# Two-layer hybrid attention trunk: up products with both halves of the hidden rows in one matmul, compression copies for two groups, first transposes in the output banks

## The chip, the cores and the metric

The kernel runs on one core of one Trainium2 chip. The metric is the device time of one execution in microseconds; lower is better.

## What is computed

Two layers (DEPTH = 2) over 256 tokens of width 1024, float32 in and out. Each layer has two attention mixers that share one input projection, a merge, and a gated feed-forward block with a causal convolution of width 3 after its up projection:

```python
def hybrid_layer(x, positions, ...):
    h = rms_norm(x, attn_pre_gain)
    u = h @ w_in
    (qa, ka, va, qb, kcb, vcb, ksb, vsb, kwb, vwb, g_nsa, g_a, g_b) = jnp.split(u, offsets, axis=-1)
    o_a = swa_sink_attention(qa, ka, va, attn_sinks)          # rotary qa, ka; window 128
    kc = compress(kcb, ...); vc = compress(vcb, ...)           # blocks of 32 rows, stride 16, small MLP
    o_b = nsa_attention(qb_raw, qb_rot, kc, vc, ks, vs, kw, vw, gates)
    mixed = jax.nn.sigmoid(g_a) * (o_a @ w_branch_a) + jax.nn.sigmoid(g_b) * (o_b @ w_branch_b)
    x = x + rms_norm(mixed @ w_out, attn_post_gain)
    h = rms_norm(x, ffn_pre_gain)
    return x + rms_norm(conv_ffn(h, ffn_w_up, ffn_conv_w, ffn_conv_b, ffn_w_down), ffn_post_gain)

def conv_ffn(h, w_up, conv_w, conv_b, w_down):
    u = h @ w_up                                               # 1024 -> 2 x 2816
    c = conv_b + sum of conv_w[k] * (u shifted by 2 - k tokens)
    a, val = jnp.split(c, 2, axis=-1)
    return (jax.nn.gelu(a, approximate=True) * val) @ w_down
```

## The kernel before

**Numbers in two parts.** Each operand of a large product is split into a high part in the matmul's rounded float32 format (`wh`, `hh`, `gh`) and a low part, the rest (`wl`, `hl`, `gl`). A product is the sum of three: high by high, high by low, low by high (`mm3`, lines 388 to 390, and the three matmuls of `up`, lines 1065 to 1067). ACT makes a high part by a copy (helper `copy`, line 114), DVE the low part by a subtraction (helper `sub`, line 117). The weights stream from memory through `Stream`: a staging tile `st`, then `wh` and `wl`, with four slots each; `W.next` hands out the next weight and makes those a little ahead.

**Order.** The program is written with a scheduler that orders each engine's instructions on a modelled time, by the order in which they are written, and that sets all waits; some stretches (`manual_schedule`) keep the written order. Work that comes between products is put off by ticks: `later(n, fn)` calls `fn` n products later, with the delays in `DL` and `PLAN`. Each engine runs its own instructions strictly in their order.

**PSUM.** Eight banks in four tags of two: `mm`, `T`, `S` and `O`. Projections use `mm` and `S`, transposes `T`, scores `S`, the attention outputs (`values`, tiles `OB`) and one token block of the down product `O`.

**Attention.** `in_tile` makes the projection in nine column tiles, for two blocks of 128 tokens (`t`); when a block of a tile is done a `fin_...` function takes it over. `q_rot`, `q_raw` and `k_rot` make stacks `stk` with high and low parts (with the rotary embedding by `rope`), and `stack_T` transposes a stack on PE into a `T` bank, four matmuls on line 515, from where ACT copies it to qA, qB, qR, kA, kS or kW. `fin_c` copies the rows to be compressed to `kvd`, one copy for keys and one for values; `cmp_blocks` transposes them (line 728) into one `T` bank and makes high and low parts in `M`, for two parities and two groups `g`: four ACT copies and four DVE subtractions for keys and as many for values. `cmp_hidden` multiplies `M` with the compression weights (line 760). `Unit.scores` (line 637), `probs_T` (line 676) and `values` (lines 708 to 710) are the attention proper; `out_T` splits an output into `OT`. Queries, outputs `OT` and the hidden pair `hp` of the feed-forward block share the tag `q8` with three buffers; the tile of one early weight uses it too.

**Feed-forward.** There are 22 pairs `j` of 128 gate and 128 value columns. Pairs 0 and 1 are made in another way (`up_first`). From pair 2 on, `up(j, half, ...)` makes the 128 columns of one half for all 256 tokens in half a bank, 24 matmuls of 256 columns; `act_gate(j)` makes the convolution (`conv`: one ACT operation, line 1048, and two DVE operations, lines 1051 and 1052), the gelu, the product (line 1073) and its high and low parts `gh`, `gl`; `down(j - 2, t)` adds the pair two before to the result. The tiles of 256 columns come from the tag `k1` with eleven buffers. In layer 0 the last pairs also make weights of the next layer (`early`).

Of the kernel before, what the change touches and what calls it, by code (L numbers as in the profile page):

```python
# [16 lines left out]
P = 128  # L17
# [35 lines left out]
DL = {'qa0': 2, 'qa1': 13, 'ka': 6, 'qb0': 8, 'qr0': 8, 'qb1': 2, 'qr1': 4, 'cb0': 1, 'cb1': 3, 'ks': 1, 'kw': 6, 'pT': (3, 3, 2), 'pv': 4, 'hT': 1, 'ge': 3, 'pj': 4, 'cT': 5, 'cv': 9, 'yT': 1, 'h0': 5, 'h1': 4, 'uf': 0, 'x0': 3, 'x1': 3}  # L53
WARM = (6, 2, 3)
FIRST = [(0, 0), (1, 0), (0, 1), (1, 1), (0, 2), (1, 2), (0, 3), (1, 3)]
EARLY = {4: ("sg", 2), 6: ("sg", 2), 8: ("kB", 1)}
# [9 lines left out]
def tile_hybrid_trunk(  # L66
# [146 lines left out]

    TAGS = {"kB": 1, "sg": 2, "q8": 3}
    W = Stream()
# [227 lines left out]
    def attn_layer(l, xp, rs, gains, first, order, last_T):  # L443
# [66 lines left out]

        def stack_T(stk, dst, key, n):
            def fn():
                b = bank("T")
                for h in range(4):
                    pe.transpose(b[:, h * P:(h + 1) * P].bitcast(F32R), stk[:, h * P:(h + 1) * P], ident_r)
                copy(dst, b.rearrange("p (h c) -> p h c", h=4) if n == 0 else b.rearrange("p (g s c) -> p g s c", g=2, s=2))
                done.add(key)
            return fn

        def q_rot(qT, t, h0, src, key, delays, exp_after=None):  # L520
            d = rope(src, t, True, 4 * len(delays))
            for i, delay in enumerate(delays):
                stk = k2(F32R)
                sv = stk.rearrange("p (h a d) -> p h a d", h=4, a=2)
                di = d[:, 4 * i:4 * i + 4, :]
                hi = copy(sv[:, :, 0, :], di)
                if exp_after is not None:
                    with tc.issue_after(hi.ins):
                        table(exp_after)
                    exp_after = None  # L530
                sub(sv[:, :, 1, :], di, r32(sv[:, :, 0, :]))
                h = h0 + 4 * i
                later(delay, stack_T(stk, qT[:, h:h + 4, t * P:(t + 1) * P], (key[0], t, h // 4), 0))

# [10 lines left out]
        def k_rot(t, src, dsts):  # L545
            d = rope(src, t, False, 2 * len(dsts))
            for i, (kT, key, delay) in enumerate(dsts):
                stk = k2(F32R)
                sv = stk.rearrange("p (g s a d) -> p g s a d", g=2, s=2, a=2)
                kb = d[:, 2 * i:2 * i + 2, None, :].to_broadcast([P, 2, 2, 64])  # L550
                copy(sv[:, :, 0], kb)
                sub(sv[:, :, 1], kb, r32(sv[:, :, 0]))
                later(delay, stack_T(stk, kT[:, :, :, t * P:(t + 1) * P], key, 1))

# [7 lines left out]

        qA, qB, qR = big8("q8", 3), big8("q8", 3), big8("q8", 3)
        kA = ap_.tile([P, 2, 2, T], F32R, tag="kA", name=nm("kA"))
# [20 lines left out]
        def fin_c(t, b):  # L585
            q_rot(qB, t, 4, heads(b, 0, 4), ("qB", t, 1), (DL["qb1"],))
            q_raw(qR, t, 4, heads(b, 0, 4), ("qR", t, 1), DL["qr1"])
            for kd in range(2):
                kvd[t][kd] = k2()
                dv = kvd[t][kd][:, 0:256].rearrange("p (g a d) -> p g a d", g=2, a=2)  # L590
                src = heads(b, 256 + kd * 128, 2)
                copy(dv, src[:, :, None, :].to_broadcast([P, 2, 2, 64]), scale=rs[t])
            if t == 1:
                later(DL["cb0"], lambda: cmp_blocks(0))
                later(DL["cb1"], lambda: cmp_blocks(1))
# [116 lines left out]
        def out_T(br, g):  # L712
            if OT[br] is None:
                OT[br] = big8("q8", 3)
            bv = OB[br][g].rearrange("p (k c) -> p k c", k=2)
            ho = OT[br][:, g * 2:g * 2 + 2, :]
            copy(ho, bv)
            sub(OT[br][:, 4 + g * 2:6 + g * 2, :], bv, r32(ho))


        def cmp_blocks(kd):
# [4 lines left out]
            for g in range(2):  # L726
                for t in range(2):
                    pe.transpose(b[:, (g * 2 + t) * P:(g * 2 + t + 1) * P], kvd[t][kd][:, g * P:(g + 1) * P], ident)
            bv = b.rearrange("p (g c pr two) -> p two pr g c", g=2, c=16, two=2)
            for par in range(2):  # L730
                rr = slice(par * 64, par * 64 + 64)
                for g in range(2):
                    ho = M[rr, :, 0:16, g]
                    copy(ho, bv[rr, par, :, g, :])
                    sub(M[rr, :, 0:16, 3 + g], bv[rr, par, :, g, :], r32(ho))
            o = R_POS + (l * 2 + kd) * 16
# [224 lines left out]
        branch(1)  # L961
        return yp

    def out_layer(l, yp, gains, order):
        gains["ffn_pre"] = gain_tile(ffn_pre_gain, l)
# [29 lines left out]
        for k in range(1, 8):  # L995
            if k < 6:
                W.make(first + k + 2)
            product(0, [k])
        hp = big8("q8", 3), big8("q8", 3)
        g, r = norm_a(res[0], gp)  # L1000
# [26 lines left out]
        scaled(1, r)  # L1027
        return hp, [lambda: t4_of(xg[1], hp, 1, 0), lambda: (t4_of(xg[1], hp, 1, 1), low())]


    def ffn_layer(l, hp, gains, last, order, last_T):
        hh, hl = hp
        gains["ffn_post"] = gain_tile(ffn_post_gain, l)
# [10 lines left out]

        def conv(b, jj, half, then=None):
            c = k1()
            u = b[:, half * T:(half + 1) * T]
            act.activation(c, u, AF.Identity, bias=cb(l, jj), scale=cw(l, 2, jj))
            if then:
                then()  # L1050
            dve.scalar_tensor_tensor(c[:, 1:T], u[:, 0:T - 1], cw(l, 1, jj), c[:, 1:T], ALU.mult, ALU.add)
            dve.scalar_tensor_tensor(c[:, 2:T], u[:, 0:T - 2], cw(l, 0, jj), c[:, 2:T], ALU.mult, ALU.add)
            return c

        up_bank, up_w, gs, wdn = {}, {}, {}, {}

        def up(j, half, c0, c1):
# [11 lines left out]
        def act_gate(j):  # L1069
            b = up_bank.pop(j)  # L1070
            ca, cv = conv(b, j, 0), conv(b, 22 + j, 1)
            act.activation(ca, ca, AF.Gelu_apprx_tanh)
# [58 lines left out]
        for j in range(2, NJ - 1):  # L1131
            for half in range(2):
                part(lambda: up(j, half, 0, T))
            act_gate(j)
# [12 lines left out]
        part(lambda: up(j, 0, 0, T))  # L1147
        ca = conv(up_bank.pop(j), j, 0)
        act.activation(ca, ca, AF.Gelu_apprx_tanh)
        up_bank[j] = bank("mm")  # L1150
        part(lambda: up(j, 1, 0, T))
        nxt = None if last else [early[l + 1, "in", c] for c in range(4)]
        cv = conv(up_bank.pop(j), 22 + j, 1, None if last else lambda: lows.append(W.high(nxt[2])))
        dve.tensor_tensor(ca, ca, cv, ALU.mult)
# [103 lines left out]
    for l in range(DEPTH):  # L1258

        yp = attn_layer(l, xp, rs, gains, l == 0, order, last_T)  # L1260
        hp, last_T = out_layer(l, yp, gains, order)
        xp, rs, last_T = ffn_layer(l, hp, gains, l == DEPTH - 1, order, last_T)
    idle(50)
# [78 lines left out]
```

## Time and profile before

| | us |
|---|---|
| median of 3 runs | 775.21 |
| lowest and highest | 775.03, 776.46 |
| the profiled execution | 774.85 |
| its span, first to last instruction | 772.8 |

In the profiled execution the span is 772.8 us of the 774.85; the rest lies around it. The busy times of the engines over the span are:

| engine | busy us | share | instructions |
|---|---|---|---|
| PE (matmul) | 756.8 | 98% | 4742 |
| PEld (weight load) | 677.0 | 88% | 4742 |
| DVE | 611.1 | 79% | 1181 |
| ACT | 497.9 | 64% | 951 |
| POOL | 26.9 | 3% | 52 |

All times of the trace are counted from the start of the span. In time order it holds, per layer, the attention stage (in layer 0 until about 165 us), the branch products, merge and output projection (until about 200 us), and the feed-forward block (until about 392 us); layer 1 follows in the same way. Matmuls are pipelined: one matmul's duration overlaps the next one's, so the pitch from start to start tells what a matmul costs, not its duration.

### The profile page before, as it was taken

To read this page: it belongs to the slowest core of one execution; us is meant where nothing else is said; L and a number is where in the kernel's file an instruction comes from. 1 tells how busy PE (TensorE), PEld (TensorE's weight loads), DVE (VectorE), ACT (ScalarE), POOL (GpSimd) and SP (SyncE) were. 2 spreads that over 40 slices of the span, in tenths; PEclk is the share of its full clock that TensorE was granted. 3 is DMA by queue.
4 is the path that set the end of the run, shared out by engine and by line. 5 is a ranking of instruction groups with operands and counts; after the bars stand their busy time and mean duration, and the time that the engine had idled before them with its cause. 6 is when DMAs were issued, how large, how long until landed. Compare 5 with 4: busy or idle time off the path is not lost.

```text
span 772.8 us, 12863 instructions
## 1 busy us (share of the span) xinstructions
PE 756.8 (98%) x4742; PEld 677.0 (88%) x4742; DVE 611.1 (79%) x1181; ACT 497.9 (64%) x951; POOL 26.9 (3%) x52
## 2 busy tenths in 40 slices
PE   8999999999999999999999999999999999999995
PEld 6888898888899999999878889988888999999994
DVE  7998898687687777777787989985967877777774
ACT  6686986755665555665566979776565655566552
POOL 3000001000000000000010000010010000000000
PEclk9999999999999999999999999999999999999998
DMA  8633265355655556766335224644655656566621
GB/s 333 198 107 122 63 205 190 137 179 178 195 202 182 187 189 191 230 221 209 132 131 157 89 79 136 210 149 148 206 189 163 185 184 191 185 192 219 196 82 55
DMA packets 42345, 131.25 MB, mean 170 GB/s; under 512 B 5375, under 2 KB 5931, under 8 KB 42283
## 3 DMA queue, kind: packets, MB, share of 16 engines
q1 hardware_dynamic: 41707, 129.39, 51.6%
q10 hardware_dynamic: 576, 1.05, 0.4%
q8 instruction: 37, 0.61, 0.3%
q14 instruction: 25, 0.20, 0.1%
HBM read 129.37 MB, written 1.05 MB: 169 GB/s over the span
## 4 chain that ended last, share of the span: by engine, by line
PE 86%; ACT 8%; DVE 3%; issue 1%; DMA 1%; POOL 0%; SPq 0%; DVEq 0%; POOLq 0%; ACTq 0%
PE mm L388 6%; PE mm L389 6%; PE mm L390 6%; PE S L388 5%; PE S L390 5%; PE S L389 5%; PE mm L1067 5%; PE mm L1066 5%; PE mm L1065 5%; PE T L1066 5%; PE T L1065 5%; PE T L1067 5%; PE O L389 4%; PE O L388 4%; PE O L390 4%; ACT k L649 2%
## 5 line engine op out<-in xcount | busy, mean ns | idle before, releaser
L117 DVE TENSOR_TENSOR wl<-st,wh 128x1024 fp32r<-128x1024 f32 (+2 forms) x214 | 253.2, 1184 | 89.4 <-ACT wh L114 86.8
L114 ACT ACTIVATE wh<-st 128x1024 fp32r<-128x1024 f32 (+2 forms) x214 | 219.1, 1027 | 158.1 <-PE mm L1066 36.8
L1065 PE MATMUL mm<-q,wh 128*128 128x256 f32 x336 | 95.1, 283 | 0.0
L1067 PE MATMUL mm<-q,wl 128*128 128x256 f32 x336 | 95.0, 283 | 0.0
L1066 PE MATMUL mm<-q,wh 128*128 128x256 f32 x336 | 95.0, 283 | 0.0
L388 PE MATMUL mm<-wh,x 128*128 128x512 f32 (+2 forms) x240 | 89.8, 374 | 0.1
L389 PE MATMUL mm<-wl,x 128*128 128x512 f32 (+2 forms) x240 | 88.2, 368 | 0.0
L390 PE MATMUL mm<-wh,x 128*128 128x512 f32 (+2 forms) x240 | 88.0, 367 | 0.0
L1066 PE MATMUL T<-q,wh 128*128 128x256 f32 x304 | 86.0, 283 | 0.0
L1067 PE MATMUL T<-q,wl 128*128 128x256 f32 x304 | 86.0, 283 | 0.0
L1065 PE MATMUL T<-q,wh 128*128 128x256 f32 x304 | 85.9, 283 | 0.0
L1065 PEld LDWEIGHTS mm<-q,wh 128*128 128x128 f32 x336 | 64.4, 192 | 0.9
L1066 PEld LDWEIGHTS mm<-q,wh 128*128 128x128 f32 x336 | 64.4, 192 | 0.8
L1067 PEld LDWEIGHTS mm<-q,wl 128*128 128x128 f32 x336 | 64.4, 192 | 0.1
L1065 PEld LDWEIGHTS T<-q,wh 128*128 128x128 f32 x304 | 58.3, 192 | 0.8
L1066 PEld LDWEIGHTS T<-q,wh 128*128 128x128 f32 x304 | 58.3, 192 | 0.7
L1067 PEld LDWEIGHTS T<-q,wl 128*128 128x128 f32 x304 | 58.3, 192 | 0.0
L390 PEld LDWEIGHTS mm<-wh,x 128*128 128x128 f32 x240 | 45.1, 188 | 5.7 <-DVE x L117 0.4
L388 PEld LDWEIGHTS mm<-wh,x 128*128 128x128 f32 x240 | 45.2, 188 | 4.8 <-ACT k L114 0.4
L389 PEld LDWEIGHTS mm<-wl,x 128*128 128x128 f32 x240 | 45.2, 188 | 4.5
L649 ACT ACTIVATE k<-k,mn 128x128 f32<-128x128 f32 (+1 forms) x96 | 42.4, 445 | 7.1 <-DVE mn L646 7.0
L114 ACT ACTIVATE k<-k 128x256 fp32r<-128x256 f32 x72 | 29.1, 413 | 13.0 <-DVE k L1073 6.1
(336 smaller groups left out, 1665.4 us busy)
## 6 DMA issues: line engine op xcount, KB each, us to landing
st<-in_ffn_w_up_dram SPq DMA_DIRECT2D x88, 512.0 KB, 4.0
st<-in_ffn_w_down_dram SPq DMA_DIRECT2D x44, 512.0 KB, 3.6
st<-in_w_in_dram SPq DMA_DIRECT2D x42, 512.0 KB, 3.8
st<-in_w_out_dram SPq DMA_DIRECT2D x16, 512.0 KB, 3.6
st<-in_w_in_dram SPq DMA_DIRECT2D x16, 384.0 KB, 3.2
st<-in_cmp_w_dram SPq DMA_DIRECT2D x16, 256.0 KB, 2.7
st<-in_w_branch_a_dram SPq DMA_DIRECT2D x8, 512.0 KB, 3.5
st<-in_w_branch_b_dram SPq DMA_DIRECT2D x8, 512.0 KB, 3.5
```

The source lines that it names most:

```text
L114: return act.activation(dst, src, AF.Copy, scale=scale)
L117: return dve.tensor_tensor(dst, a, b, ALU.subtract)
L388: pe.matmul(o, xh, wh, start=first, stop=False, skip_group_check=True)
L389: pe.matmul(o, xh, wl, start=False, stop=False, skip_group_check=True)
L390: pe.matmul(o, xl, wh, start=False, stop=last, skip_group_check=True)
L649: last_exp[0] = act.activation(self.pt[:, hh, s, :], sm[:, :nk], AF.Exp, bias=self.mn[:, i:i + 1], scale=-1.0, accum_out=self.dn[:, i:i + 1])
L1065: pe.matmul(o, wh[:, k, :], hh[:, k, c0:c1], start=(k == 0), stop=False, skip_group_check=True)
L1066: pe.matmul(o, wh[:, k, :], hl[:, k, c0:c1], start=False, stop=False, skip_group_check=True)
L1067: pe.matmul(o, wl[:, k, :], hh[:, k, c0:c1], start=False, stop=(k == 7), skip_group_check=True)
```

## The change

The diff has four parts.

1. For the pairs in `JOINT` (2 to 16) `up_joint` takes the place of `up`: the hidden pair lies in one tile `H` with both parts next to each other, one matmul multiplies `wh` with both parts (512 columns, the second half of the bank is the low part's product), and one adds `wl` by `hh` to the first half. `left` then copies the second half out with ACT and adds the first half with DVE; `conv` reads this sum. Each half of a pair takes a bank of its own, `mm` for even and `T` for odd pairs.
2. `H` (tag `h16`, one buffer) holds qA and qB, then `OT[0]` and `OT[1]`, then the hidden pair; the tag `q8` keeps one buffer.
3. `stack_T` takes the bank's tag: the transposes of qA, of qB's first four heads, of kA and of kS use `O` in place of `T`.
4. `fin_c` copies keys and values of a token block in one ACT copy; `cmp_blocks` makes each high and low part for both groups in one operation.

```diff
+JOINT = range(2, 17)
-    TAGS = {"kB": 1, "sg": 2, "q8": 3}
+    TAGS = {"kB": 1, "sg": 2, "q8": 1}
-        def stack_T(stk, dst, key, n):
+        def stack_T(stk, dst, key, n, tag="T"):
             def fn():
-                b = bank("T")
+                b = bank(tag)
...
-                later(delay, stack_T(stk, qT[:, h:h + 4, t * P:(t + 1) * P], (key[0], t, h // 4), 0))
+                later(delay, stack_T(stk, qT[:, h:h + 4, t * P:(t + 1) * P], (key[0], t, h // 4), 0, "T" if h0 else "O"))
...
-                later(delay, stack_T(stk, kT[:, :, :, t * P:(t + 1) * P], key, 1))
+                later(delay, stack_T(stk, kT[:, :, :, t * P:(t + 1) * P], key, 1, "T" if key[0] == "kW" else "O"))
...
-        qA, qB, qR = big8("q8", 3), big8("q8", 3), big8("q8", 3)
+        H = ap_.tile([P, 2, KD, T], F32R, tag="h16", name=nm("H"))
+        qA, qB, qR = H[:, 0], H[:, 1], big8("q8", 1)
...
-            for kd in range(2):
-                kvd[t][kd] = k2()
-                dv = kvd[t][kd][:, 0:256].rearrange("p (g a d) -> p g a d", g=2, a=2)
-                src = heads(b, 256 + kd * 128, 2)
-                copy(dv, src[:, :, None, :].to_broadcast([P, 2, 2, 64]), scale=rs[t])
+            both = k2()
+            copy(both.rearrange("p (g a d) -> p g a d", g=4, a=2), heads(b, 256, 4)[:, :, None, :].to_broadcast([P, 4, 2, 64]), scale=rs[t])
+            kvd[t] = both[:, 0:256], both[:, 256:512]
...
-                OT[br] = big8("q8", 3)
+                OT[br] = H[:, br]
...
-            bv = b.rearrange("p (g c pr two) -> p two pr g c", g=2, c=16, two=2)
+            bv = b.rearrange("p (g c pr two) -> p two pr c g", g=2, c=16, two=2)
             for par in range(2):
                 rr = slice(par * 64, par * 64 + 64)
-                for g in range(2):
-                    ho = M[rr, :, 0:16, g]
-                    copy(ho, bv[rr, par, :, g, :])
-                    sub(M[rr, :, 0:16, 3 + g], bv[rr, par, :, g, :], r32(ho))
+                ho = M[rr, :, 0:16, 0:2]
+                copy(ho, bv[rr, par])
+                sub(M[rr, :, 0:16, 3:5], bv[rr, par], r32(ho))
...
-        hp = big8("q8", 3), big8("q8", 3)
+        hp = H[:, 0], H[:, 1]
...
-        def conv(b, jj, half, then=None):
+        def conv(u, jj, then=None):
             c = k1()
-            u = b[:, half * T:(half + 1) * T]
...
+        def up_joint(j, half):
+            b = up_bank[j, half] = bank("mm" if j % 2 == 0 else "T")
+            wh, wl, _ = W.next(8, P)
+            both = b.rearrange("p (s t) -> p s t", s=2)
+            for k in range(8):
+                pe.matmul(both, wh[:, k, :], H[:, :, k, :], start=(k == 0), stop=False, skip_group_check=True)
+                pe.matmul(b[:, 0:T], wl[:, k, :], hh[:, k, :], start=False, stop=(k == 7), skip_group_check=True)
+
+        def left(j, half):
+            if j not in JOINT:
+                return up_bank[j][:, half * T:(half + 1) * T]
+            b = up_bank.pop((j, half))
+            u = k1()
+            copy(u, b[:, T:2 * T])
+            dve.tensor_tensor(u, b[:, 0:T], u, ALU.add)
+            return u
...
-            b = up_bank.pop(j)
-            ca, cv = conv(b, j, 0), conv(b, 22 + j, 1)
+            ua, uv = left(j, 0), left(j, 1)
+            ca, cv = conv(ua, j), conv(uv, 22 + j)
...
-                part(lambda: up(j, half, 0, T))
+                part(lambda: up_joint(j, half) if j in JOINT else up(j, half, 0, T))
```

## Rows read from the trace of the kernel before

**Rows 1.** The page: span, busy times, and the chain that ended last by engine.
```profile
span 772.8 us, 12863 instructions
...
PE 756.8 (98%) x4742; PEld 677.0 (88%) x4742; DVE 611.1 (79%) x1181; ACT 497.9 (64%) x951; POOL 26.9 (3%) x52
...
PE 86%; ACT 8%; DVE 3%; issue 1%; DMA 1%; POOL 0%; SPq 0%; DVEq 0%; POOLq 0%; ACTq 0%
```

**Rows 2.** Busy time per engine in three stretches: a pair, late pairs, attention.
```profile
core 0: us, PE busy (x) PEld busy (x) DVE busy (x) ACT busy (x) POOL busy (x), PEclk, DMA share, GB/s
260.86:269.39 8.53, 8.53 (x61) 8.01 (x60) 6.20 (x10) 4.79 (x7) 0.00 (x0) 1.00 0.58 184
337.50:346.50 9.00, 9.00 (x66) 8.44 (x65) 7.47 (x11) 5.81 (x9) 0.00 (x0) 1.00 0.78 242
...
45.00:165.00 120.00, 117.59 (x740) 105.43 (x738) 102.34 (x283) 91.80 (x227) 3.94 (x4) 1.00 0.42 138
```

**Rows 3.** PE in order of time: one pair's edges (start, duration, line, tiles, shape).
```profile
260.64 0.39 PE L390 MATMUL O<-wh,k 128*128 128x512 f32 x1
260.86 0.28 PE L1065 MATMUL T<-q,wh 128*128 128x256 f32 x1
...
266.62 0.39 PE L388 MATMUL S<-wh,k 128*128 128x512 f32 x1
...
269.16 0.39 PE L390 MATMUL O<-wh,k 128*128 128x512 f32 x1
269.39 0.28 PE L1065 MATMUL T<-q,wh 128*128 128x256 f32 x1
```

**Rows 4.** PE in order of time: scores that read two separate runs.
```profile
74.90 1.11 PE L637 MATMUL S<-kB,q 128*128 128x256 f32 x8
75.85 0.40 PE L388 MATMUL mm<-wh,x 128*128 128x512 f32 x1
```

**Rows 5.** Groups of ACT and DVE by shape: busy us, mean ns, idle before.
```profile
L1048 ACT ACTIVATE k<-mm,vec 128x256 f32<-128x256 f32 x42 | 23.1, 550 | 2.3 <-DVE k L1052 2.1
...
L114 ACT ACTIVATE M<-T 64x128 fp32r<-64x128 f32 x16 | 6.4, 401 | 0.2
...
L114 ACT ACTIVATE SG<-mm,rstd 128x512 f32<-128x512 f32 x8 | 5.4, 680 | 3.0 <-PE mm L390 3.0
...
L114 ACT ACTIVATE k<-mm,rstd 128x256 f32<-128x256 f32 x8 | 3.3, 466 | 0.0
...
L1051 DVE SCALAR_TENSOR_TENSOR k<-mm,vec,k 128x255 f32<-128x255 f32 x42 | 20.0, 477 | 2.0 <-ACT k L1048 2.0
...
L1073 DVE TENSOR_TENSOR k<-k,k 128x256 f32<-128x256 f32 x42 | 17.9, 426 | 4.4
```

**Rows 6.** ACT and DVE in order of time: one weight's two parts, with waits.
```profile
261.06 1.06 ACT L114 ACTIVATE wh<-st 128x1024 fp32r<-128x1024 f32 x1 [1.38 <-PE O L390]
...
262.15 1.23 DVE L117 TENSOR_TENSOR wl<-st,wh 128x1024 fp32r<-128x1024 f32 x1 [0.75 <-ACT wh L114]
```

**Rows 7.** What PE waited for: us in total, times, longest.
```profile
PE T L515 <- ACT k L114: 1.5, 2, 0.8
...
PE T L515 <- ACT q L114: 1.2, 2, 0.6
...
PE T L515 <- DVE M L117: 1.0, 2, 0.5
...
PE T L728 <- ACT k L114: 0.5, 2, 0.2
PE T L676 <- DVE M L117: 0.3, 2, 0.2
```

**Rows 8.** Order of time in the attention stage: two waits, and the compression copies.
```profile
50.81 0.28 PE L515 MATMUL T<-ident_r,k 128*128 128x128 f32 x1 [0.78 <-ACT k L114]
...
84.07 0.41 ACT L114 ACTIVATE M<-T 64x128 fp32r<-64x128 f32 x1
...
88.61 0.40 DVE L117 TENSOR_TENSOR M<-T,M 64x128 fp32r<-64x128 f32 x1 [0.32 <-ACT M L114]
...
89.06 0.53 PE L515 MATMUL T<-ident_r,k 128*128 128x128 f32 x4 [0.50 <-DVE M L117]
```

More of the change, by code (lines that the diff above doesn't have):

```diff
@@ L961, in attn_layer, with out_layer @@
         branch(1)
-        return yp
-    def out_layer(l, yp, gains, order):
+        return yp, H
+    def out_layer(l, yp, H, gains, order):
         gains["ffn_pre"] = gain_tile(ffn_pre_gain, l)
@@ L1027, in out_layer, with ffn_layer @@
         scaled(1, r)
-        return hp, [lambda: t4_of(xg[1], hp, 1, 0), lambda: (t4_of(xg[1], hp, 1, 1), low())]
-    def ffn_layer(l, hp, gains, last, order, last_T):
-        hh, hl = hp
+        return [lambda: t4_of(xg[1], hp, 1, 0), lambda: (t4_of(xg[1], hp, 1, 1), low())]
+    def ffn_layer(l, H, gains, last, order, last_T):
+        hh, hl = hp = H[:, 0], H[:, 1]
         gains["ffn_post"] = gain_tile(ffn_post_gain, l)
@@ L1147, in ffn_layer @@
         part(lambda: up(j, 0, 0, T))
-        ca = conv(up_bank.pop(j), j, 0)
+        ca = conv(left(j, 0), j)
         act.activation(ca, ca, AF.Gelu_apprx_tanh)
@@ L1152, in ffn_layer @@
         nxt = None if last else [early[l + 1, "in", c] for c in range(4)]
-        cv = conv(up_bank.pop(j), 22 + j, 1, None if last else lambda: lows.append(W.high(nxt[2])))
+        cv = conv(left(j, 1), 22 + j, None if last else lambda: lows.append(W.high(nxt[2])))
         dve.tensor_tensor(ca, ca, cv, ALU.mult)
@@ L1258, in tile_hybrid_trunk @@
     for l in range(DEPTH):
-        yp = attn_layer(l, xp, rs, gains, l == 0, order, last_T)
-        hp, last_T = out_layer(l, yp, gains, order)
-        xp, rs, last_T = ffn_layer(l, hp, gains, l == DEPTH - 1, order, last_T)
+        yp, H = attn_layer(l, xp, rs, gains, l == 0, order, last_T)
+        last_T = out_layer(l, yp, H, gains, order)
+        xp, rs, last_T = ffn_layer(l, H, gains, l == DEPTH - 1, order, last_T)
     idle(50)
```

## Prediction

> **What bounds the kernel now.** I read the page first. PE is busy for 756.8 of 772.8 us, and the chain that ended last is PE for 86% of its length, ACT 8%, DVE 3% [rows 1]. So only two things can shorten the run: fewer or closer matmuls, or less of the 16.0 us in which PE stands still. Next I read the stretches. One steady pair of the up/down loop (260.86 to 269.39) has PE busy for all of its 8.53 us at full granted clock, with DVE busy 6.20 and ACT 4.79; there every nanosecond taken off a matmul's pitch is a nanosecond of the run [rows 2]. The first attention stage (45 to 165) has 117.59 of 120 busy, so at most 2.4 us per layer can come from its waits [rows 2]. Third, the list of who PE waited for: copies and subtractions around the transposes, 4.5 us together [rows 7].
>
> **Joint up products: PE.** Per step of `k` the old loop issues three 256-column matmuls, each with its own weight load: wh with hh, wh with hl, wl with hh. The new one issues one 512-column matmul (wh over hh and hl) and one of 256 columns, so the columns stay 768 and one matmul and one load go. What is saved is only what a matmul costs beyond its columns. The 48 up matmuls of a pair start between 260.86 and 266.62, 5.76/48 = 0.120 each [rows 3]. The twelve 512-column matmuls of the two downs run from 266.62 to 269.39, 2.77/12 = 0.231 each, and the last one before an up matmul takes 0.22 to 0.23 [rows 3], say 0.227. Twice the columns thus cost 0.107 to 0.111 more, and the rest of a 256-column pitch, 9 to 13 ns, is paid per matmul, whatever its columns. A step is 3 x 0.120 = 0.360 now and 0.227 + 0.120 = 0.347 (to 0.231 + 0.120 = 0.351) afterwards: 9 to 13 ns saved; I take 12, because in the new step each 512-column matmul is followed by a 256-column one, as in the rows at 260.64 and 269.16. Pairs 2 to 16 are 15, times two halves, two layers and 8 steps: 480 steps, so **-5.8 us**, bounds -4.3 and -6.2.
>
> The moving operand of the joint matmul is two runs of 256 columns that lie apart (H is laid out as halves, then `k`). The scores against kB already read two separate runs of 128: eight of them take 75.85 - 74.90 = 0.95 us, 0.119 each, no more than a contiguous 256 [rows 4]. So I cost the jump at nothing; if every run were paid like a matmul of its own, that is the first rival.
>
> A rule that speaks against this part: the Trainium skill, "TensorE: Matmul & The Clock Gate", section "Back-to-back issue gap", gives N/2.4 plus 2.5 ns when warm. By it a step would fall from 327.5 to 325 ns, an estimate of 1.2 us for 480 steps in place of 5.8. The rows have 120 for 256 columns where it gives 109, so this case's own pitch decides.
>
> **Joint up products: ACT and DVE.** `left` adds, for each half, one ACT copy of 256 columns out of PSUM and one DVE add. The nearest copy is 466 ns, and the nearest add (L1073, both inputs in SBUF) 426 ns [rows 5]; an add with one input in PSUM lies between that and the 477 of L1051 [rows 5]. Per pair that is 2 x 0.47 = 0.93 us more on ACT (5.7 of a new pair time of 8.53 - 16 x 0.012 = 8.34) and 2 x 0.45 = 0.9 on DVE (7.1 of 8.34). The conv's own operations (550 on ACT, 477 on DVE, now reading SBUF instead of PSUM) may get a little cheaper; I take no change [rows 5]. So neither engine is filled in a steady pair. Where next-layer weights are made too (337.5 to 346.5), DVE has 7.47 of 9.00 [rows 2]; with 0.9 more in a pair it comes close to full for the last three joint pairs of layer 0.
>
> What hides the additions is a lead in the weights. The wh copy that starts at 261.06 waited for a slot of the four to come free at the end of the downs; its wl is done at 262.15 + 1.23 = 263.38 [rows 6]. Three weights are then still ahead of it (the pair in use and one down), so PE wants it at 269.39 [rows 3]: a lead of 6.0 us. The gate has even more: its gh and gl are used two pairs later. Queued behind the new instructions are the next wh copies on ACT and the next wl on DVE; they may slip by up to 6 us before PE waits. If that cover goes, the price is the second rival.
>
> Buffers: each half has its own bank now, so a pair holds two of `mm` or both of `T`, and they are wanted again two pairs (17 us) later; the old rotation came round after four. They are read within one pair, so PE does not wait. A pair takes six k1 buffers in place of four, of eleven; gh and gl of two pairs plus the pair being made are ten at most. H is the same 16 KB as two q8 buffers, used in the same order (queries, branch outputs, hidden pair), and the one q8 that is left serves qR and the early weights as before. Nothing of the DMA queues changes. These go together at 0.
>
> **Transposes in the output banks.** The T transposes of qA, of the first half of qB, of kA and kS move to the O banks, which stand empty until the first values. That removes waits for a T bank's copy: L515 waited 1.2 us on q copies, over two layers [rows 7]. But right behind it stands another wait that no bank ends: at 50.81 PE waited 0.78 us for the k stack of kS [rows 8], which ACT and DVE make in their own order, so what PE gains before may be waited again. Bounds 0 and -1.2; I take -0.4.
>
> **Compression rows.** `fin_c` copies 512 columns at once where it copied 256 twice (466 each) [rows 5]; the nearest 512-column copy with a scale takes 680 [rows 5], so 0.25 us less ACT per token block, 1.0 us in all; but the first transpose needs only the first half of it, and may start 0.2 us later per layer. `cmp_blocks` makes 16 ACT copies of 64x128 (401 ns [rows 5]) and as many DVE subtractions in the two layers; half as many with twice the columns remain. At the 466 of the 256-column copy that is 16 x 0.40 - 8 x 0.47 = 2.6 us less ACT; DVE saves about the same. All of it lies off PE, and counts only where PE waits. It does: the four copies of one block come from 84.07 on, with other ACT work between them, the last subtraction is at 88.61, and all that time one T bank is held; PE waits 0.50 us for it at 89.06 [rows 8]. These waits (DVE M: 1.0 and 0.3 over both layers [rows 7]) should go: -1.3, less 0.4 for the later first transpose, and some 0.6 for a shorter ACT queue: **-1.5**, bounds +1.5 (the scheduler of the program re-orders this crowded stage) and -3.3 (all L515, L676 and L728 waits, 4.5, less the 1.2 above).
>
> **The tail of layer 0.** Pairs 17 to 21 are not joint and keep their ACT and DVE work, and PE paces both there by the slots it frees; PE and the last gate come earlier together. No change.
>
> **Sum.** -5.8 - 0.4 - 1.5 = -7.7 us against the profiled execution, 774.85 us with a span of 772.8. That gives 767.15; that execution lies 0.36 below the median of the runs, inside their spread, so I predict **767.2**. Bounds of this case: -4.3 + 0 + 1.5 gives 772.1, -6.2 - 1.2 - 3.3 gives 764.1.
>
> **Rivals.** First: the joint matmul saves nothing, because what costs beyond the columns is paid per run of 256, so a step stays 0.360. Only the attention part stays: 774.85 - 1.9 = 773.0. For it speaks that 512 columns cost 0.231 and not 0.227 within the downs; against it speak the two-run scores [rows 3, 4]. Chance 0.11. By the rule of the Trainium skill named above, "TensorE: Matmul & The Clock Gate", "Back-to-back issue gap", the time would be an estimated 774.85 - 1.2 - 1.9 = 771.8, near this rival.
>
> Second, the other side: in the pair loop ACT and DVE hand each half to and fro (copy, add, conv, two multiply-adds, in queues that keep their order), and this chain becomes longer than PE's pair. In program order the chain on DVE is wl 1.23, add 0.43, conv on ACT 0.55, multiply-adds 2 x 0.48, all that once more, the gate product 0.43, the third wl 1.23 and gl 0.43: 8.4 us [rows 5, 6], against PE's 8.34. That alone is covered by the lead. It decides from a pair time of 8.34 + 6.0/15 = 8.74 on. If one of the present waits of DVE for wh (0.75 at 262.15 [rows 6]) stays in the chain, a pair is 9.15: (9.15 - 8.34) x 15 - 6.0 = 6.1 us lost per layer, 12.2 in all, so 767.2 + 12.2 = 779.4, slower than before. Against it: those waits exist because ACT waits for slots that PE frees (1.38 at 261.06 [rows 6]), and shrink when ACT is late. Chance 0.13.
>
> Third: the loop gains, and the attention stage gets a worse order than its bound of +1.5, by some 3 us: 774.85 - 5.8 + 3 = 772.1 to 774. Chance 0.06.
>
> **Chances and range.** Forecast 0.70. A measurement of this kernel can tell about 0.2%, 1.6 us, from no change, so faster means below 773.6: the forecast, most of the first rival, a part of the third: 0.80. Within 0.2%: 0.07. Slower: the second, 0.13. The range goes from the forecast's 764.1 to the first rival's 773.0 and some 0.3 beyond.
>
> **What would show it.** In the new profile: joint matmuls 0.227 to 0.231 before the next start and 0.120 for the wl one; a pair of some 8.34 us with PE full; DVE near 7.1 us in it; weights still finished microseconds before use; L515 and L676 waits on M and q gone; the k waits left. Wrong would be: PE waits for wl or wh in pairs 2 to 16, a 512-column pitch near 0.24, or new waits on O banks before the first values.

## The result and the profile after

The changed kernel takes 770.86 us (median of 4 executions, 769.76 to 771.82) against 775.12 for the kernel before on the same chip (4, 774.74 to 776.46): ratio 0.9944 [0.9929, 0.9959]. It is 4.3 us faster where 7.9 were forecast (767.2); the time lies in the range given, on its slow side. The profiled execution is the slowest of the four, 771.82 us with a span of 769.9.

The page of the changed kernel, as in [rows 1]: 480 matmuls are gone (4262 for 4742), PE's busy time fell by only 2.1 us, and DVE has 14.1 us more to do, ACT 13.9.

```profile
span 769.9 us, 12095 instructions
...
PE 754.7 (98%) x4262; PEld 653.0 (85%) x4262; DVE 625.2 (81%) x1233; ACT 511.8 (66%) x999; POOL 26.9 (3%) x52
...
PE 88%; ACT 6%; DVE 4%; issue 1%; POOL 0%; DMA 0%; DVEq 0%; POOLq 0%; SPq 0%; ACTq 0%
```

Busy time per engine of the changed kernel in three stretches (columns as in [rows 2]): a steady pair, a stretch of late pairs, the first attention stage.

```profile
262.07:270.51 8.44, 8.44 (x46) 7.17 (x45) 6.70 (x13) 5.32 (x9) 0.00 (x0) 1.00 0.56 188
339.00:347.50 8.50, 8.50 (x62) 7.99 (x61) 8.06 (x13) 6.50 (x11) 0.00 (x0) 1.00 0.71 239
46.50:166.50 120.00, 117.33 (x735) 104.73 (x734) 101.54 (x279) 90.74 (x221) 3.91 (x4) 1.00 0.42 137
```

PE fills the steady pair as before. In the late pairs DVE is busy for 8.06 of 8.50 us, where [rows 2] had 7.47 of 9.00. The attention stage has not gained: PE is busy for 117.33 of 120 us there, before it was 117.59 with other edges.

PE of the changed kernel in order of time, two pairs (answering [rows 3]):

```profile
262.06 0.39 PE L1063 MATMUL mm<-H,wh 128*128 128x512 f32 x1
262.29 0.28 PE L1064 MATMUL mm<-H,wl 128*128 128x256 f32 x1
262.40 0.40 PE L1063 MATMUL mm<-H,wh 128*128 128x512 f32 x1
...
267.71 0.39 PE L389 MATMUL S<-wh,k 128*128 128x512 f32 x1
...
270.50 0.40 PE L1063 MATMUL T<-H,wh 128*128 128x512 f32 x1
...
276.06 0.39 PE L389 MATMUL S<-wh,k 128*128 128x512 f32 x1
...
278.83 0.39 PE L1063 MATMUL mm<-H,wh 128*128 128x512 f32 x1
```

The pairs take 8.44 and 8.33 us in turn, 8.39 in the mean, for 8.53 before. Their 16 joint steps take 5.65 us and 5.56, so 0.353 and 0.348 each. Over all steps of the trace the 512-column matmul takes 0.234 to the next start and the 256-column one 0.117: 0.351 for 0.360, 9 ns saved.

What PE waited for in the changed kernel (us in total, times, longest), answering [rows 7]:

```profile
PE O L517 <- ACT k L115: 2.9, 4, 0.7
...
PE T L730 <- ACT k L115: 1.0, 2, 0.5
PE T L678 <- DVE k L672: 0.9, 3, 0.4
PE T L1240 <- DMA k<-in_attn_pre_gain_dram: 0.5, 1, 0.5
PE T L678 <- ACT SG L115: 0.3, 1, 0.3
```

The waits on q and on M are gone, as forecast. But the wait for the stacks' copies has grown from 1.5 to 2.9 us, the one of the compression transposes (L728, now L730) from 0.5 to 1.0, and two are new (L678). The sum is no smaller. In order of time these are two of the first kind in layer 0, where [rows 8] had one of 0.78:

```profile
48.05 0.28 PE L517 MATMUL O<-ident_r,k 128*128 128x128 f32 x1 [0.70 <-ACT k L115]
...
52.32 0.28 PE L517 MATMUL O<-ident_r,k 128*128 128x128 f32 x1 [0.74 <-ACT k L115]
```

By the positions of the first transpose, the first compressed score and the up matmuls in the two traces, the profiled difference of 2.9 us in span is made of: the opening +1.5, the two attention stages +0.6, the two up/down loops -1.9 each, and the 8 us after the last matmul -1.2. The opening is this execution's alone (a gain vector landed 0.5 us later, L1240 above, and matmuls stay slow for longer behind it: three of 512 columns at 7.54 take 1.63 us, in the kernel before at 6.45 they take 0.94); the other kernels that hold the same code there open in 25.9 to 26.4 us, the kernel before in 26.1. The -1.2 at the very end was in nobody's sum.

Costs of the new and changed operations in the changed kernel (columns as in [rows 5]):

```profile
L1072 DVE TENSOR_TENSOR k<-mm,k 128x256 f32<-128x256 f32 x32 | 12.0, 416 | 0.0
...
L115 ACT ACTIVATE k<-mm 128x256 f32<-128x256 f32 x32 | 10.2, 368 | 0.0
...
L115 ACT ACTIVATE M<-T 64x256 fp32r<-64x256 f32 x8 | 3.6, 455 | 0.5 <-PE T L730 0.4
...
L115 ACT ACTIVATE k<-mm,rstd 128x512 f32<-128x512 f32 x4 | 2.7, 681 | 0.6 <-DVE k L544 0.6
```

The copy of `left` takes 0.37 us and its add 0.42; the estimates were 0.47 and 0.45. The copies of M (455) and of `fin_c` (681) cost what was put down for them.

### The profile page after: what moved, and what is told of

The parts are those of the page before. It is cut to its first block, busy times and chain, and to the rows that moved or that the text cites. A ratio compares the mean times of both kernels' runs of the same rounds, so it can differ in the third digit from the quotient of the medians.

```text
span 769.9 us, 12095 instructions
## 1 busy us (share of the span) xinstructions
PE 754.7 (98%) x4262; PEld 653.0 (85%) x4262; DVE 625.2 (81%) x1233; ACT 511.8 (66%) x999; POOL 26.9 (3%) x52
## 3 DMA queue, kind: packets, MB, share of 16 engines
q1 hardware_dynamic: 41707, 129.39, 50.7%
## 4 chain that ended last, share of the span: by engine, by line
PE 88%; ACT 6%; DVE 4%; issue 1%; POOL 0%; DMA 0%; DVEq 0%; POOLq 0%; SPq 0%; ACTq 0%
PE mm L1063 8%; PE T L1063 7%; PE mm L389 7%; PE mm L391 6%; PE mm L390 6%; PE S L389 5%; PE S L391 5%; PE S L390 5%; PE mm L1064 4%; PE O L390 4%; PE O L389 4%; PE O L391 4%; PE T L1064 3%; PE T L678 2%; PE S L639 2%; ACT k L651 2%
## 5 line engine op out<-in xcount | busy, mean ns | idle before, releaser
L1063 PE MATMUL mm<-H,wh 128*128 128x512 f32 x256 | 91.3, 399 | 0.0
L389 PE MATMUL mm<-wh,x 128*128 128x512 f32 (+2 forms) x240 | 90.9, 379 | 0.0
L1063 PE MATMUL T<-H,wh 128*128 128x512 f32 x224 | 78.7, 393 | 0.0
L1064 PE MATMUL mm<-H,wl 128*128 128x256 f32 x256 | 71.9, 281 | 0.0
L1064 PE MATMUL T<-H,wl 128*128 128x256 f32 x224 | 62.8, 280 | 0.0
L1063 PEld LDWEIGHTS mm<-H,wh 128*128 128x128 f32 x256 | 48.2, 188 | 11.7
L1063 PEld LDWEIGHTS T<-H,wh 128*128 128x128 f32 x224 | 42.0, 187 | 9.4
L1064 PEld LDWEIGHTS mm<-H,wl 128*128 128x128 f32 x256 | 48.4, 189 | 0.6
L389 PEld LDWEIGHTS mm<-wh,x 128*128 128x128 f32 x240 | 45.2, 188 | 4.2
L1064 PEld LDWEIGHTS T<-H,wl 128*128 128x128 f32 x224 | 42.4, 189 | 0.8
L1048 ACT ACTIVATE k<-k,vec 128x256 f32<-128x256 f32 x60 | 32.4, 587 | 2.2 <-DVE k L1072 2.2
L389 PE MATMUL S<-wh,k 128*128 128x512 f32 x80 | 31.7, 397 | 0.0
```

The lines of the kernel that those rows point to most:

```text
L389: pe.matmul(o, xh, wh, start=first, stop=False, skip_group_check=True)
L1063: pe.matmul(both, wh[:, k, :], H[:, :, k, :], start=(k == 0), stop=False, skip_group_check=True)
L1064: pe.matmul(b[:, 0:T], wl[:, k, :], hh[:, k, :], start=False, stop=(k == 7), skip_group_check=True)
```

## The experiments

The ratio's interval is given where it decides; the kernel before, measured beside them in three groups of runs, took 774.85 to 774.97.

**1 to 4. The parts apart.** First the joint products alone (with tile `H`), `fin_c`, `cmp_blocks` and the banks as before:

```
-            both = k2()
-            copy(both.rearrange(...), heads(b, 256, 4)..., scale=rs[t])
+            for kd in range(2):
+                kvd[t][kd] = k2()
...
-                ho = M[rr, :, 0:16, 0:2]
+                for g in range(2):
+                    ho = M[rr, :, 0:16, g]
...
-                later(delay, stack_T(..., "T" if h0 else "O"))
+                later(delay, stack_T(..., "T"))
```

> Joint up products and the H tile alone: transposes back in T, compression rows as in the kernel before. Theory A (the loop gives all of the gain, at 9.2 ns a step, 480 x 9.2 ns = 4.4 us, less some 0.5 us at the seams of the loop): 775.1 - 3.9 = 771.2, as fast as the whole change within 0.5 us. Theory B (the prediction's sizes, 5.8 us for the loop, and the rest of the change costs 1.5 us): 769.3, faster than the whole change. Theory C (part of the gain comes from the attention stage): 772 or more.

Measured 769.91 us (769.68 to 769.97), ratio 0.9937 [0.9923, 0.9950]. This is some 0.9 us faster than the whole change, and runs 2 and 3 agree: the attention edits lose time. It is nearest to the expectation of 769.3, but not for its reason. That took 5.8 us for the loops; in this trace they gain 4.0, and 1.2 more come at the end of the run (run 10).

Second, the attention edits and tile `H` with no joint pair:

```
-JOINT = range(2, 17)
+JOINT = range(0)
```

> No joint pair (range is empty): only the H tile, the transposes in the output banks and the merged compression rows stay. Theory A (the attention stage is set by ACT and DVE in their order; a wait that is removed is waited for later): same as before or up to 0.6 us slower, 775.1 to 775.7, with the waits on q and M gone and longer waits on the k stacks. The prediction's sizes: 1.9 us faster, 773.2. Theory C: 0.5 to 1 us faster.

Measured 774.70 (773.88 to 775.95), ratio 0.9998 [0.9989, 1.0007]. Nothing is left of the 1.9 us that the prediction gave to these edits, though this kernel has the shorter end too (run 10).

Third, only the banks undone (compression rows and joint products stay), and fourth, only the compression rows undone (banks and joint products stay); the edits are those of the first diff.

> The whole change, but all transposes in T again; joint pairs and merged compression rows stay. If the output banks are worth nothing by themselves: the time of the whole change, 770.9. If they cost 0.3 us per layer: 770.3. If they hide a loss of the rows (their own worth 0.5 us per layer): 771.9.

> The whole change, but with the compression rows copied and split as in the kernel before; joint pairs and output banks stay. If the merged rows are worth nothing: 770.9. If the later first transpose of the compression (its wait grew from 0.2 to 0.5 us per layer) is a loss that the shorter copies do not give back: 770.3. If the merged rows gain what the prediction put (1.5 us): 772.4.

Measured 770.87 (770.02 to 771.84) and 770.05 (769.88 to 770.42). So the banks are worth nothing, with the rows (770.87 against 770.86) or without them (770.05 against 769.91), and the merged rows cost some 1.0 us (770.87 against 769.91) and spread the executions over 2 us. Why the banks give nothing stands in the waits of the kernel with the rows undone:

```profile
PE O L517 <- ACT k L115: 2.9, 4, 0.7
...
PE T L517 <- DVE M L118: 1.0, 2, 0.5
```

L517's waits are 3.9 us, and L515's were 1.5 + 1.2 + 1.0 = 3.7 in [rows 7]. The bank was free sooner, but the stack to be transposed was not: the 1.2 us gained from q were waited again for ACT's copies.

**5. One matmul or two.** The joint products with the 512-column matmul cut in two; the banks, `left` and `H` stay:

```
-                pe.matmul(both, wh[:, k, :], H[:, :, k, :], ...)
+                pe.matmul(b[:, 0:T], wh[:, k, :], hh[:, k, :], ...)
+                pe.matmul(b[:, T:2 * T], wh[:, k, :], hl[:, k, :], ...)
```

> joint_only with the one merged matmul undone: wh by hh and wh by hl are two matmuls of 256 columns again, but into the same two halves of a bank of its own, with the same copy and add in left. Theory A (the gain is the merged matmul, 9.2 ns a step): 480 x 9.2 ns = 4.4 us slower than joint_only, 774.3, a pitch of 0.120 for all three. Rival (the gain comes from the banks, the earlier conv or the H tile): 769.9 to 771.

Measured 773.50 (773.34 to 773.90), ratio 0.9980 [0.9971, 0.9989], 3.6 us over the first run. Its pair, in order of time on PE:

```profile
260.82 0.28 PE L1066 MATMUL mm<-H,wh 128*128 128x256 f32 x1
260.93 0.28 PE L1067 MATMUL mm<-H,wh 128*128 128x256 f32 x1
261.05 0.28 PE L1068 MATMUL mm<-H,wl 128*128 128x256 f32 x1
...
269.35 0.28 PE L1066 MATMUL T<-H,wh 128*128 128x256 f32 x1
```

The pair is back at 8.53 and the loop at 165.96 us per layer, as before the change. So all of the loop's gain is the matmul that is gone, and the added copies, adds and banks cost the loop nothing. The remaining 1.5 us to the kernel before lie at the end of the run, to its larger part at least (run 10).

**6. The jump in the moving operand.** `H` laid out so that both parts of a `k` lie side by side:

```
-        H = ap_.tile([P, 2, KD, T], F32R, tag="h16", name=nm("H"))
+        H = ap_.tile([P, KD, 2, T], F32R, tag="h16", name=nm("H"))
```

> joint_only with H laid out as k, part, token, so that the 512 moving columns of a joint matmul lie in one run. Theory D (the jump between the two runs is why a joint matmul takes 0.234 in place of the forecast 0.227): 3 to 7 ns less per step, 480 steps, 1.4 to 3.4 us faster than joint_only, 766.5 to 768.5. Theory E (the pitch of a 512-column matmul is 0.230 to 0.234 wherever other engines work beside it): 769.9 as joint_only, pitch unchanged.

Measured 770.93 (769.51 to 771.21); the loops take 164.05 us per layer, for 164.05 and 163.92 in the first run. Two runs of 256 cost no more than one of 512, so the first rival's mechanism is out, and the jump is not why the pitch is 0.234. The 1.0 us by which this run is slower than the first does not come from the loops. In its trace PE waits 0.79 us for a k stack at 50.9, and the granted clock is at its lower level from there until 54.3 (third number from the right):

```profile
52.00:54.00 2.00, 2.00 (x12) 1.99 (x11) 1.42 (x9) 1.16 (x5) 0.00 (x0) 0.50 0.00 0
```

The first run's trace has the same wait (0.78) and no such drop.

**7. How thick the cover is.** `left` done twice:

```
             u = k1()
-            copy(u, b[:, T:2 * T])
-            dve.tensor_tensor(u, b[:, 0:T], u, ALU.add)
+            for _ in range(2):
+                copy(u, b[:, T:2 * T])
+                dve.tensor_tensor(u, b[:, 0:T], u, ALU.add)
```

> joint_only with the copy and the add of left made twice, the second time over the first: 0.37 more ACT and 0.42 more DVE per half. Theory A (the lead of the weights covers ACT and DVE work): no change, 769.9, at most 0.5 more at the end of layer 0. Second rival of the prediction (the hand-over between ACT and DVE nearly bounds the pair): DVE comes to 7.8 of 8.3 us per pair, the chain lengthens by 2 x 0.8, and 15 pairs x 1.2 us less 6 us of lead per layer are lost: 780 or more.

Measured 789.48 (788.63 to 791.88), ratio 1.0189 [1.0172, 1.0207]. A pair's work on ACT grew by 0.74 us and on DVE by 0.84, well below the lead of 6 us that the prediction relied on, yet the loops lost 10 and 12 us. First the cover as it is in the changed kernel; ACT and DVE in order of time, beside the PE rows above:

```profile
266.23 0.64 ACT L115 ACTIVATE k<-T 128x256 f32<-128x256 f32 x2
267.79 1.06 ACT L115 ACTIVATE wh<-st 128x1024 fp32r<-128x1024 f32 x1 [0.93 <-PE mm L1063]
...
267.50 0.75 DVE L1072 TENSOR_TENSOR k<-T,k 128x256 f32<-128x256 f32 x2
```

Banks T hold the pair of 253.7 to 259.3. They are copied only at 266.23, since ACT and DVE work well behind PE, and set free by the two adds, which the row shows as one. Each half has its own bank; the first add takes 0.42 us, so the first bank is free at 267.92. PE starts the next pair in it at 270.50: the bank's lead is 2.6 us (2.5 to 2.8 in 14 of the 15 pairs of layer 0, 2.0 in the first), and the second half's bank is wanted later still. With `left` done twice, the second pair of adds and PE's start:

```profile
269.25 0.75 DVE L1076 TENSOR_TENSOR k<-T,k 128x256 f32<-128x256 f32 x2
...
269.81 0.47 PE L1066 MATMUL T<-H,wh 128*128 128x512 f32 x1
```

The second copies and adds queue behind the first ones and weight work, so the add that frees the first bank starts 2.5 us after the first of its kind (269.25 for 266.76) and ends at 269.67. PE starts 0.14 us later. The lead is gone, and from the first pairs on the banks pace PE (8.51 to 8.61 us per pair). Where weights of the next layer are made as well, it stalls, and the clock falls behind the stall (PE in order of time, then the stretches):

```profile
323.88 0.47 PE L1066 MATMUL T<-H,wh 128*128 128x512 f32 x1 [2.56 <-DVE k L1076]
...
324.82 0.63 PE L1066 MATMUL T<-H,wh 128*128 128x512 f32 x1
...
325.46 0.63 PE L1066 MATMUL T<-H,wh 128*128 128x512 f32 x1
```

```profile
318.00:323.80 5.80, 3.32 (x16) 2.41 (x14) 4.00 (x8) 4.18 (x8) 0.00 (x0) 1.00 0.83 259
323.80:328.00 4.20, 4.12 (x15) 3.52 (x16) 3.40 (x7) 1.48 (x3) 0.00 (x0) 0.59 0.72 202
```

A step takes 0.64 us in place of 0.35 (324.82 to 325.46): after a stall of 2.6 us the granted clock is 0.59 of 2.4 GHz in the mean of 4.2 us, at its 1.2 GHz level for the larger part of them, so by estimate some 1.7 us are lost on top. The longest stall is in layer 1, where no weights of a next layer are made, and it is not for a bank. ACT waits for a staging transfer, a gate's copy stands behind it, and PE waits for that gate, with the lower clock for 6 us behind it (ACT, PE, stretch):

```profile
716.51 1.06 ACT L115 ACTIVATE sg<-st 128x1024 fp32r<-128x1024 f32 x1 [3.13 <-DMA st<-in_ffn_w_down_dram]
...
717.92 0.79 PE L389 MATMUL S<-wh,k 128*128 128x512 f32 x1 [3.10 <-ACT k L115]
...
717.90:723.80 5.90, 5.88 (x14) 4.62 (x15) 3.48 (x6) 2.20 (x5) 0.00 (x0) 0.50 0.53 169
```

By the same estimate this is 3.1 + 3.0, half of what layer 1 lost.

**8 and 12. More joint pairs.** The first run's kernel with pairs 2 to 20:

```
-JOINT = range(2, 17)
+JOINT = range(2, 21)
```

> joint_only with the joint pairs 2 to 20 in place of 2 to 16. Theory A: 4 pairs x 2 halves x 8 steps x 2 layers = 128 steps x 9.2 ns = 1.2 us faster than joint_only, 768.7. Rival (layer 0 makes next-layer weights in pairs 14 to 17, DVE is near full there, and its backlog then delays the last gate): layer 1 gains 0.6, layer 0 loses as much or more, 769.9 to 771.

Measured 774.81 (774.04 to 776.29), ratio 0.9996 [0.9987, 1.0005]: five microseconds worse than pairs 2 to 16, worse than either expectation. The pairs 17 to 20 do take 8.33 and 8.44, but then PE stands:

```profile
372.64 0.39 PE L1086 MATMUL mm<-H,wh 128*128 128x256 f32 x1 [2.50 <-DVE k L1075]
```

This is the second half of pair 21, which wants a bank of `mm` that pair 20 still holds. So the last run gave it a bank of T:

```
-        up_bank[j] = bank("mm")
+        up_bank[j] = bank("T")
```

> Joint products for pairs 2 to 20, old compression rows and banks, as in the run more_joint (774.81), and the second half of pair 21 in bank T in place of mm. Theory B (in more_joint the loss is pair 21's wait of 2.5 us for a bank of mm that pair 20 still held, with a lower clock behind it and late weights of the next layer): the wait goes, pairs 17 to 20 take 8.38 us in place of 8.53, layer 1's attention stage is back at 114.8, time 768.7 to 769.5. Rival (the work of left in the pairs that also make the next layer's weights fills DVE and ACT): the wait moves to weights or to another bank, 772 or more.

Measured 775.40 (774.48 to 777.46), ratio 1.0006 [0.9997, 1.0015]. The wait has moved, not gone. PE and ACT of this run in order of time, then ACT of the first run for the same gate, the last one:

```profile
380.34 0.59 PE L389 MATMUL S<-sg,k 128*128 128x512 f32 x1 [2.72 <-ACT k L115]
```

```profile
379.88 0.42 ACT L115 ACTIVATE k<-k 128x256 fp32r<-128x256 f32 x1 [0.58 <-DVE k L1175]
```

```profile
377.25 0.42 ACT L115 ACTIVATE k<-k 128x256 fp32r<-128x256 f32 x1 [0.57 <-DVE k L1175]
```

So it was not the bank but the queue. At the end of the loop PE has no later pairs to go on with: it needs the gate of pair 21, ACT and DVE do pair 20's copies and adds first, and the gate comes 2.6 us later. The bank theory falls. The rival (ACT and DVE are filled) holds, but the wait is for a gate, where the rival put it at weights or another bank, and its place is the end of the loop. The wait is half of the loss of 5.5 us. Behind it the granted clock is 0.54 for 3.7 us, by estimate 1.7 us more, and in the next layer's attention stage PE waits 1.0 us for `z`, which it does not in the first run:

```profile
380.30:384.00 3.70, 3.66 (x9) 2.87 (x10) 3.48 (x5) 2.31 (x5) 0.11 (x1) 0.54 0.27 72
...
PE T L680 <- DVE z L789: 1.0, 1, 1.0
```

**9 and 11. Which half of the compression rows.** The first run's kernel with `fin_c` alone merged, and with `cmp_blocks` alone merged (each is half of the first diff):

> The joint products with fin_c's merged copy alone (old cmp_blocks, old banks). Both edits on the compression rows together cost 0.9 us over the joint products alone (770.87 against 769.91) and spread the runs over 2 us. Theory F (the wider fin_c copy moves ACT's order, so that weight copies come early and wait for their staging transfer): 770.6 to 771.0, spread over 1.5 us or more. Theory G (cmp_blocks' merged copies do it, through the order of DVE's subtractions): 769.9, spread under 0.6 us.

> The joint products with cmp_blocks' merged copies alone (old fin_c, old banks). Theory F (fin_c does it): 769.9 or, if the 1.0 us of waits on M in the kernel before is gained here, down to 768.9, spread under 0.6 us. Theory G (cmp_blocks does it): 770.6 to 771.0, spread over 1.5 us or more.

`fin_c` alone: 772.48 (771.57 to 773.40), 2.6 us slower than without it and beyond both expectations. `cmp_blocks` alone: 770.14 (768.78 to 771.65). What PE waited for with `fin_c` alone:

```profile
PE O L710 <- ACT k L115: 1.1, 2, 0.5
...
PE T L730 <- ACT k L115: 0.9, 2, 0.5
PE mm L389 <- ACT wh L115: 0.8, 2, 0.4
```

The waits of L710 and L389 are new and that of L730 had been 0.5: 2.3 us. One of 0.5 us for L678 is new as well, and the M waits (1.0 and 0.5 us in the first run's trace) are gone here too. The net is 1.3 us of the 1.8 by which this span is longer than the first run's (770.0 for 768.2); the rest was not followed. One operation of 0.68 us has to be done before the first transpose where the first of two did, and behind it ACT's order is another: a weight copy and a probability copy come after PE wants them. With `cmp_blocks` alone the M waits (1.3 us in [rows 7]) are gone, as forecast; only 0.6 for L680 on SG is new. Two of its five executions take 768.8 and 768.9, with a mean clock of 0.999, and the other three 770.1 to 771.7 with 0.995 to 0.997. The profiled one is of the second kind, and shows where:

```profile
48.00:50.00 2.00, 1.95 (x17) 1.73 (x16) 1.68 (x9) 2.00 (x10) 0.00 (x0) 1.00 0.00 0
50.00:52.00 2.00, 1.28 (x6) 1.28 (x7) 1.99 (x10) 1.92 (x7) 0.00 (x0) 0.64 0.00 0
52.00:54.00 2.00, 2.00 (x11) 1.99 (x11) 1.24 (x9) 1.24 (x5) 0.00 (x0) 0.50 0.00 0
```

After the wait of 0.77 us at 50.7 the clock is at its lower level, 0.50, until 54, as in run 6. In the first run's trace the same wait of 0.78 us (at 51.1) has no such drop. So `cmp_blocks` gains 1.0 us where the clock stays and loses it where it does not; Theory F stands for the cost, but its sign of a wide spread was found here too. The two halves do not add up (2.6 and 0.2 alone, 1.0 together); which order of ACT's queue makes the difference was not followed further.

**10. The end of the run.** The kernel before, with eight small instructions more on ACT (the expectation counts the one that was there, too) and twelve on DVE at its start:

```
     table(AF.Sin)
+    for _ in range(8):
+        table(AF.Sin)
...
         dve.memset(r32(z), 0.0)
+        for _ in range(12):
+            dve.memset(small("shift", 1, 1), 0.0)
```

> The kernel before, with nine small instructions more on ACT and twelve on DVE at the very start, where both wait for data. All kernels run so far end 1.2 us sooner after the last DVE operation than the kernel before: in its trace one 8 KB piece of program code is fetched at 770.1, among the packets of the last output transfer, whose landing takes 3.2 us in place of 2.0. Theory L (where the pieces of code fall decides): the shifted kernel fetches no code among the last output packets, landing 2.0 us, time 773.7 (773.5 to 773.9) with the rest of the run unchanged. Theory M (the tile H or another place in memory makes the output faster): nothing changes, 774.9, and the landing stays at 3.2 us.

Measured 773.80 (773.58 to 775.02) against 774.85, ratio 0.9988 [0.9979, 0.9997]. The DMA view of the last 6 us of the kernel before (a queue of program code: packets, MB, share; then the output's issues: count, KB each, median us to landing), then of the changed kernel and of this one, which have no packets of code there:

```profile
q14 instruction: 1, 0.01, 0.3%
...
out_dram<-X SPq DMA_DIRECT2D x2, 256.0 KB, 3.2
```

```profile
out_dram<-X SPq DMA_DIRECT2D x2, 256.0 KB, 2.0
```

```profile
out_dram<-X SPq DMA_DIRECT2D x2, 256.0 KB, 2.0
```

Twenty instructions that do nothing make the kernel before 1.1 us faster. In its trace one piece of program code is fetched while the last output goes out, which lands 1.2 us later; in no other trace of this study is code fetched among the last output packets. That the fetch delays the output is inferred from these traces; that it is not the tile `H` is shown, since this kernel has none.

## Why the prediction was right or wrong

- **Joint products on PE:** right in mechanism, mis-sized. The step that failed is "I take 12": the 512-column matmul was put at 0.227, from its one place before an up matmul, and takes 0.234; the one of 256 columns takes 0.117, not 0.120. That is 9 ns for 12, and the lower bound of 4.3 us was the better number. The loops gained 3.8 us in the change and 4.0 in the first run: pairs 4 to 16 give 1.8 or 1.9 us per layer, 0.14 each, and pairs 2 and 3 only 0.1 in place of 0.3, around the transposes and new weights between their products. The pitch lies between the signs given, 0.227 to 0.231 for right and 0.24 for wrong; why it is 0.234 in this neighbourhood was not followed. By the Trainium skill, "TensorE: Matmul & The Clock Gate", section "Back-to-back issue gap", whose formula is for an isolated matmul, it would have been an estimated 1.2 us; the measurement is 3.6 (run 5), so what a matmul costs beyond its columns is more here than that rule has.
- **ACT and DVE at nothing:** right for pairs 2 to 16 (run 5), for a reason that was wrong. The step "they are read within one pair, so PE does not wait" failed: the banks are read 7 us after their last matmul, and the shortest cover of the additions is the first bank's 2.6 us, not the weights' 6.0. The second rival counted with those 6.0 us; it decides much earlier, at once when `left` costs twice as much (run 7). The pace of the pairs is then set by the bank; the longest single wait is for a gate, and a stall costs the clock as well. Its sign was right: slower, 789.5.
- **Transposes in the output banks:** -0.4 forecast, 0.0 measured (runs 1, 3 and 4). The doubt stated with it, that what is gained may be waited again for the k stack, is what happened.
- **Compression rows:** -1.5 forecast, +1.0 measured, inside the bounds (-3.3 to +1.5) with the wrong sign. The M waits went as forecast, though not by `cmp_blocks` alone, since `fin_c` alone removes them too (run 9). The step that failed is "0.4 for the later first transpose, and some 0.6 for a shorter ACT queue". A shorter queue gave nothing back, because ACT's order changed with it: `fin_c` alone costs 2.6 us.
- **The tail of layer 0:** no change, as forecast. It holds because pairs 17 to 21 are not joint; with joint pairs up to 20 it costs some 5 us (runs 8 and 12).
- **Not in the sum:** -1.2 us at the end of the run, from where a piece of program code falls (run 10).

Together: 1.9 us less from the joint products, 2.5 from the rows and 0.4 from the banks, less the 1.2 found at the end, is 3.6 of the 3.7 us by which the forecast missed. That it missed by no more is luck to the size of those 1.2 us, which no step of the prediction has: without them the change would stand near 772.1, the slow bound of the sum. The first rival is out (run 6). The third (a worse order in the attention stage, within 772 to 774) had the right place and a smaller size. The fastest kernel by its median is the joint products alone, 769.91.

## What to carry to other kernels

Price a merged matmul by its pitch in the neighbourhood it will have, and take the cautious end where the saving is nanoseconds times hundreds. For work added to an engine that is not the bound, look for the shortest lead and not the largest: find when a PSUM bank's last reader ends and when PE wants it next, also at the end of the loop, where PE has nothing later to go on with. Merging copies in a crowded stage moves the order of everything behind them on that engine, so count what must now be done before the first consumer.

## What the runs showed of the hardware that was not expected

- One fetch of program code (8 KB) among the last output packets goes with 1.2 us on the landing (3.2 for 2.0 us), and a change of twenty instructions moves it (774.85 to 773.80).
- A granted clock of 0.50 for over 3 us came with a wait of 0.77 us in one trace (run 11) and of 0.79 in another (run 6), and not in the first run's with the same wait at nearly the same place. In run 7 it came after a wait of 2.6 us (323.9) and not after one of 2.2 (345.5).
- A 256-column matmul takes 0.117 us behind one of 512 columns and 0.120 among its like; a moving operand in two separate runs costs nothing (run 6).
